# Squares of x summed on GpSimd, x's statistics requested earlier, and three early pieces inside the first unit, in a one-layer hybrid attention block

## The chip, the core and the metric

The kernel runs on one core of a Trainium2 chip. The metric is the device time of one execution in microseconds (us); the time shown is the median of three runs.

The core has these engines, each with a queue of its own that runs in order: TensorE (PE in the profile; its weight loads are PEld), VectorE (DVE), ScalarE (ACT), GpSimd (POOL) and SyncE (SP), which only issues the DMAs here.

## What is computed

One decoder layer for 256 tokens of 1024 features, all in float32:

```python
hn  = rmsnorm(x, g_attn)                    # mean of x*x over the features
qkv = hn @ w_in                             # 1024 x 3072: heads A, then heads B
ya  = rmsnorm(attention_a(qkv), g_out_a)    # 8 heads, dilated windows merged, ALiBi
yb  = rmsnorm(attention_b(qkv), g_out_b)    # 8 heads, causal (one block), ALiBi
h   = x + concat(ya, yb) @ w_out
h   = h + square(relu(rmsnorm(h, g_mlp) @ w_up)) @ w_down
h   = h + sigmoid(rmsnorm(h, g_ple) @ w_ple_gate + b) * (p @ w_ple_proj)
return rmsnorm(h, g_final)
```

## The kernel before

**Split operands.** Every large matmul is done with operands split in two parts, hi and lo, whose sum is the float32 value, as three matmuls: hi·hi, hi·lo, lo·hi (`mm3`, L207 to L211). A weight slab of 1 MB arrives as `raw`; ScalarE makes hi of a piece (L79), VectorE makes lo as raw minus hi (L86). A slab of the first unit has four pieces, 512 columns wide; a slab of the later attention units has two, 1024 wide. x is split in the same way into `aT` (L289 on ScalarE, L290 on VectorE).

**x's statistics.** The weights are multiplied with x not yet normalized, and the factor is applied to the products. `x_squares` squares x's eight feature blocks on ScalarE (L320, L323) and adds them up in `xsq` on VectorE (L324). `x_stats` sums over the features with small matmuls (L330), then VectorE makes the mean (L240) and GpSimd the reciprocal root (L241). `x_diag` (L339, VectorE) and `x_bcast` (L345 TensorE, L347 VectorE, L348 ScalarE) spread it over `rb`, with which q and k are multiplied when they leave PSUM.

**Order of the work.** For the attention part the order on TensorE, VectorE, ScalarE and GpSimd is the order in which the program emits the instructions (a manual schedule). A unit is a list of steps of matmuls. Its `inserts` say what is emitted after which step.
- Unit 1 of the list (here "the first unit") has 48 steps, six for each of the eight feature blocks k: two of v (0.70 us each) and four of q and k (0.36 us each). All its splits are emitted before its steps, in `first_splits`, block by block.
- The second unit (`slabs_in[2]`, 32 steps of q and k) has four pieces, made ahead of it: `early(0)` to `early(3)`. Here they are called hi(0), lo(0) to hi(3), lo(3).
- From the second unit on, a planner keeps a clock: each step adds its cost (0.36 or 0.681 us), and events (`at`, `within`) are emitted after the first step at whose end they are due. The clock is 0 at the end of the first unit. The clock places instructions in the queues; it delays none.
- While the second unit runs, the four pieces of the third (`slabs_in[5]`, called P0 to P3 here) are made; while the third runs, those of the fourth (`slabs_in[3]`, Q0 to Q3).

**One pair of heads (g, j).** `evac_qk` multiplies q and k with `rb` (mult, L362, VectorE), splits the result (qkhi L366, ScalarE; qklo L370, VectorE) and plans `scores` (L400, 12 matmuls). `scores` plans the softmax: `reduce` for each of two heads (L408, L411, VectorE: adds a table of distances and takes the maximum), `exp` for each head (L418, ScalarE), the reciprocal of the sums (L422, VectorE), `norm` (L429 on GpSimd and L431 on ScalarE), and the next pair's table, `make_bias` (L388, L390, GpSimd). It plans `turn` 7.4 after itself: six transposes (L451, TensorE), whose results are copied (L455, VectorE and ScalarE), and then `values` (L467, L468), whose result is split into y (L476, L485) and squared for the next norm (L478, L481, with an add on GpSimd, L482). The reciprocal is planned 4.7 and `norm` 4.8 after `scores`.

With n the number of the pair, scores of pair n are planned so:

```python
t = clock[0]
dt = 0.1 if n != 1 else 2.6
at(t + dt, mult)
at(t + dt + 0.7, hi)
at(t + dt + 1.4, lo)
at(max(t + dt + 3.2, 3.4 + 8.4 * n), lambda: scores(g, j), 0.75)
```

Of the kernel before, what the change touches and what calls it, by code (L numbers as in the profile page):

```python
# [10 lines left out]
F32 = mybir.dt.float32  # L11
# [3 lines left out]
ALU = mybir.AluOpType  # L15
PSUM = bass.MemoryType.PSUM

P = 128
S = 256
# [13 lines left out]
def block_kernel(ctx: ExitStack, tc: tile.TileContext, a: dict):  # L33
    nc = tc.nc
# [8 lines left out]
    def bank():  # L43
        n_ps[0] += 1
        return psum.tile([P, 512], F32, tag="ps", name=f"ps{n_ps[0]}")
# [65 lines left out]
    def at(t, f, cost=0.0):  # L111
        events.append((t, len(events), f, cost))
# [79 lines left out]
    def first_splits():  # L192
        for k in range(KT):
            if k in (0, 1, 2, 4):
                x_split(k, k + (1 if k < 2 else 2))
            sv, sq = (slabs_in[u][k // 4] for u in range(2))
            for part in (slice(0, 0.5), slice(0.5, 1)) if k == 0 else [slice(0, 1)]:
                for f in sv.halves(k % 4, part):
                    f()
            for f in sq.halves(k % 4):  # L200
                f()
            if k == 4:
                x_split(6, 8)
            if k:
                x_squares({1: range(2), 2: range(2, 4), 4: range(4, 8)}.get(k, ()))

    def mm3(ps, lhs, rhs, start, stop):  # L207

# [36 lines left out]
    ap = attn_pool.__enter__()  # L245
# [67 lines left out]
    xsq = ap.tile([P, S], F32, name="xsq")  # L313

    def x_squares(ks):

        for k in ks:
            x = x_rows(k, k + 1)[:, 0]
            if k == 0:
                nc.scalar.activation(xsq, x, AF.Square)  # L320
            else:
                sq = ap.tile([P, S], F32, tag="sq", name="sq", bufs=2)
                nc.scalar.activation(sq, x, AF.Square)  # L323
                nc.vector.tensor_tensor(xsq, xsq, sq, op=ALU.add)  # L324

    def sum_tokens(sums):

# [29 lines left out]
    def evac_qk(g, j, ps):  # L357
        d = pr[g, j] = {}

        def mult():  # L360
            d["raw"] = ap.tile([P, 2 * S], F32, tag="qk", name="qk", bufs=2)
            nc.vector.tensor_tensor(d["raw"], ps, rb, op=ALU.mult)  # L362

        def hi():
            d["hi"] = ap.tile([P, 2 * S], F32R, tag="qkhi", name="qkhi", bufs=3)
            nc.scalar.activation(d["hi"], d["raw"], AF.Copy)  # L366

        def lo():
            d["lo"] = ap.tile([P, 2 * S], F32R, tag="qklo", name="qklo", bufs=3)
            nc.vector.tensor_tensor(d["lo"], d["raw"], d["hi"].bitcast(F32), op=ALU.subtract)  # L370
            d["q"], d["k"] = ([t[:, i * S : (i + 1) * S] for t in (d["hi"], d["lo"])] for i in range(2))

        t = clock[0]
        n = NPAIR * g + j
        dt = 0.1 if n != 1 else 2.6
        at(t + dt, mult)
        at(t + dt + 0.7, hi)
        at(t + dt + 1.4, lo)
        at(max(t + dt + 3.2, 3.4 + 8.4 * n), lambda: scores(g, j), 0.75)

    biases = {}

    def make_bias(g, j):
        bias = biases[g, j] = ap.tile([P, 2, S], F32, tag="bias", name="bias", bufs=2)
        for h in range(2):
            head = 2 * j + h
            sl = SLOPES[2 * head + g]
            nc.gpsimd.tensor_scalar(bias[:, h], dist_b if g else dist_a, sl, 1.0, op0=ALU.mult, op1=ALU.mult)  # L388
            if g == 0:
                nc.gpsimd.tensor_tensor(bias[:, h], bias[:, h], logc, op=ALU.subtract)  # L390

    def scores(g, j):
        d = pr[g, j]

        ps = [bank(), bank()]
        for c, w, q0 in ((0, S, P), (S, P, 0)):
            for i, (a_, b_) in enumerate(((0, 0), (0, 1), (1, 0))):
                for h in range(2):
                    r = slice(h * HD, (h + 1) * HD)
                    last_mm[0] = nc.tensor.matmul(ps[h][:, c : c + w], d["q"][a_][r, q0 : q0 + P], d["k"][b_][r, :w],  # L400
                                                  start=i == 0, stop=i == 2)
        sc = ap.tile([P, 2, 3 * P], F32, tag="sc", name="sc", bufs=2)
        pb = d["p"] = ap.tile([P, 2, 3 * P], F32, tag="pb", name="pb", bufs=2)
        nm = ap.tile([P, 3, 4], F32, tag="nm", name="nm", bufs=3)
        parts = ((0, slice(P, 3 * P)), (1, slice(0, P)))

        def reduce(h):
            nc.vector.tensor_tensor_reduce(  # L408
                sc[:, h, P:], ps[h][:, :S], biases[g, j][:, h], 1.0, 3e38,
                op0=ALU.add, op1=ALU.min, accum_out=nm[:, 0, 2 * h : 2 * h + 1])  # L410
            nc.vector.tensor_tensor_reduce(  # L411
                sc[:, h, :P], ps[h][:, S : S + P], biases[g, j][:, h, P:], 1.0, 3e38,
                op0=ALU.add, op1=ALU.min, accum_out=nm[:, 0, 2 * h + 1 : 2 * h + 2])

        def exp(h):
            for i, sl in parts:
                c = slice(2 * h + i, 2 * h + i + 1)
                nc.scalar.activation(pb[:, h, sl], sc[:, h, sl], AF.Exp, bias=nm[:, 0, c], scale=-1.0,  # L418
                                     accum_out=nm[:, 1, c])

        def recip():
            nc.vector.reciprocal(nm[:, 2], nm[:, 1])  # L422

        def norm():
            for h in range(2):
                for i, sl in parts:
                    r = nm[:, 2, 2 * h + i : 2 * h + i + 1]
                    if i:
                        nc.gpsimd.tensor_scalar(pb[:, h, sl], pb[:, h, sl], r, 1.0, op0=ALU.mult, op1=ALU.mult)  # L429
                    else:  # L430
                        nc.scalar.activation(pb[:, h, sl], pb[:, h, sl], AF.Copy, scale=r)  # L431

        n = NPAIR * g + j
        within(0.75, lambda: reduce(0))
        within(1.4, lambda: reduce(1))
        within(1.9, lambda: exp(0))
        within(2.9, lambda: exp(1))
        within(4.7, recip)
        within(4.8, norm)
        if n < 7:  # L440
            within(0.8, lambda: make_bias((n + 1) // NPAIR, (n + 1) % NPAIR))
        within(7.4, lambda: turn(g, j), 0.7)
# [17 lines left out]
    def values(g, j):  # L460
        d = pr[g, j]
        ps = bank()
        v = vt[g]
        for h in range(2):
            cols = slice((2 * j + h) * HD, (2 * j + h + 1) * HD)
            o = ps[h * HD : (h + 1) * HD]
            nc.tensor.matmul(o[:, :S], v[:, 0, cols], d["pT"][h][:, :S], start=True, stop=False)  # L467
            last_mm[0] = nc.tensor.matmul(o[:, P:S], v[:, 1, cols], d["pT"][h][:, S:], start=False, stop=True)  # L468
        if j == 0 and g == 1:
            y1 = ap.tile([P, 2, NPAIR, S], F32R, tag="xy", name="y1")  # L470
            yT.append([y1[:, 0], y1[:, 1]])
        yh, yl = yT[g]
        gain = gv[:, 1, NPAIR * g + j : NPAIR * g + j + 1]

        def hi():
            nc.scalar.activation(yh[:, j], ps[:, :S], AF.Copy, scale=gain)  # L476
            if j == 0:
                nc.scalar.activation(ysum[g], ps[:, :S], AF.Square)  # L478
            else:
                sq = ap.tile([P, S], F32, tag="sq", name="sq", bufs=2)  # L480
                nc.scalar.activation(sq, ps[:, :S], AF.Square)  # L481
                nc.gpsimd.tensor_tensor(ysum[g], ysum[g], sq, op=ALU.add)  # L482

        def lo():
            nc.vector.scalar_tensor_tensor(yl[:, j], ps[:, :S], gain, yh[:, j].bitcast(F32),  # L485
                                           op0=ALU.mult, op1=ALU.subtract)

        within(1.0, hi)
        within(1.6, lo)
        if j == NPAIR - 1 and g == 0:  # L490
            within(3.6, lambda: y_stats(g), 0.3)
# [30 lines left out]
    def v_evac(g):  # L522
        for t in range(2):
            nc.scalar.activation(vt[g][:, t], held[g][t], AF.Copy, scale=xr["r"][:, t : t + 1])
# [45 lines left out]
    def early(n):  # L570

        return list(slabs_in[2][n // 2].halves(n % 2))
# [1 line left out]
    def b_evac():  # L574
        within(0.5, lambda: v_evac(1))

    def late_pieces():
        for n in (2, 3):
            hi, lo = early(n)
            at(1.3 * (n - 2), hi)  # L580
            at(1.3 * (n - 2) + 1.1, lo)

    units = [
        Unit(slabs_in[0] + slabs_in[1], first_steps,
             {33: [x_stats], 37: [x_diag] + early(0), 41: [x_bcast, lambda: make_bias(0, 0)], 43: early(1),
              48: [late_pieces, lambda: v_evac(0)]}),
        Unit(slabs_in[2], qk_steps(2, 0, 2), {14: [late_loads]}, 32, 0.36),
        Unit(slabs_in[5], v_steps(5, 1), {16: [b_evac]}, 16, 0.681),
        Unit(slabs_in[3], qk_steps(3, 1, 0), None, 32, 0.36),
# [313 lines left out]
```

## Time and profile before

| | us |
|---|---|
| median of three runs | 340.74 |
| lowest and highest of them | 340.59 to 340.94 |
| the profiled execution | 341.23 |
| its span in the profile | 339.4 |
| TensorE busy in it | 328.1 |

The profile is of one execution. The span is what the trace covers; the execution is 1.8 us longer than it. All instants below are microseconds from the start of the span. In a row of a timeline stand the start, the duration, the engine, the line, the operation, what is written and read, and how many instructions are merged; a bracket says how long the engine was idle before it and what ended that. Instructions that follow each other closely overlap a little in it, so the distance between starts is shorter than a duration.

### The profile page before, as it was taken

How to read it: one execution, taken by the hardware profiler on the slowest of the kernel's cores; microseconds unless marked ns; L12 is line 12 of the kernel's file. 1: busy time of each engine (PE TensorE's matmuls, PEld its weight loads, DVE VectorE, ACT ScalarE, POOL GpSimd, SP SyncE). 2: the span in 40 equal slices, each digit the busy share in tenths (PEclk: the TensorE clock that was granted, in tenths of full speed). 3: DMA queues.
4: the chain of work that ended last, by engine and by line, in shares of the span. 5: the costliest groups of instructions: out<-in, count | busy, mean ns of one | idle time of the engine just before them, and what ended most of it. 6: DMA issues, size and time to landing. Idle time of an engine off the chain costs nothing.

```text
span 339.4 us, 5168 instructions
## 1 busy us (share of the span) xinstructions
PE 328.1 (97%) x1932; PEld 281.8 (83%) x1932; DVE 233.1 (69%) x431; ACT 204.9 (60%) x400; POOL 43.1 (13%) x65
## 2 busy tenths in 40 slices
PE   8899989999999999999999999999999999999991
PEld 7789967899987788888888888888888888888890
DVE  3786987566765989879475686585755956658564
ACT  6785688847675968747364383554743836458421
POOL 0009057134122111000000000000000000000322
PEclk9999999999999999999999999999999999999997
DMA  7998883341433487735619437366193472700011
GB/s 197 358 356 289 315 280 143 112 193 50 145 136 126 140 317 245 289 126 186 250 62 322 172 109 265 126 239 254 21 352 124 146 257 95 249 0 1 2 62 62
DMA packets 10681, 60.84 MB, mean 179 GB/s; under 512 B 1184, under 2 KB 1952, under 8 KB 4128
## 3 DMA queue, kind: packets, MB, share of 16 engines
q1 hardware_dynamic: 10656, 60.51, 50.1%
q8 instruction: 15, 0.25, 0.3%
q14 instruction: 10, 0.08, 0.1%
HBM read 59.46 MB, written 1.05 MB: 178 GB/s over the span
## 4 chain that ended last, share of the span: by engine, by line
PE 84%; DVE 5%; DMA 4%; ACT 2%; issue 1%; SPq 1%; POOL 1%; POOLq 0%; DVEq 0%; ACTq 0%
PE ps L708 18%; PE ps L209 17%; PE ps L210 17%; PE ps L211 17%; PE ps L709 9%; DMA raw<-in_w_in 3%; PE ps L400 2%; DVE lo L86 2%; PE ps L451 2%; PE ps L467 1%; DMA xT<-in_xT 1%; PE ps L635 1%; DVE qklo L370 1%; ACT hi L79 1%; PE ps L468 1%
## 5 line engine op out<-in xcount | busy, mean ns | idle before, releaser
L86 DVE TENSOR_TENSOR lo<-raw,hi 128x1024 fp32r<-128x1024 f32 (+2 forms) x75 | 80.9, 1101 | 31.2 <-ACT hi L79 31.1
L708 PE MATMUL ps<-h,hi 128*128 128x512 f32 x256 | 90.9, 399 | 0.0
L79 ACT ACTIVATE hi<-raw 128x1024 fp32r<-128x1024 f32 (+2 forms) x75 | 69.3, 950 | 32.8 <-PE ps L211 27.0
L709 PE MATMUL ps<-h,lo 128*128 128x256 f32 x256 | 71.9, 281 | 0.0
L88 DVE SCALAR_TENSOR_TENSOR lo<-raw,head,hi 128x512 fp32r<-128x512 f32 x80 | 56.9, 746 | 9.6 <-ACT hi L81 9.6
L81 ACT ACTIVATE hi<-raw,head 128x512 fp32r<-128x512 f32 x80 | 52.8, 715 | 10.9 <-PE ps L211 5.5
L708 PEld LDWEIGHTS ps<-h,hi 128*128 128x128 f32 x256 | 48.1, 188 | 11.8
L209 PE MATMUL ps<-hi,u 128*128 128x512 f32 x128 | 50.3, 393 | 0.0
L211 PE MATMUL ps<-hi,u 128*128 128x512 f32 x128 | 49.9, 390 | 0.0
L210 PE MATMUL ps<-lo,u 128*128 128x512 f32 x128 | 49.9, 390 | 0.0
L709 PEld LDWEIGHTS ps<-h,lo 128*128 128x128 f32 x256 | 48.4, 189 | 0.2
L209 PE MATMUL ps<-x,hi 128*128 128x256 f32 x128 | 37.5, 293 | 0.0
L211 PE MATMUL ps<-x,lo 128*128 128x256 f32 x128 | 36.3, 283 | 0.2 <-DVE lo L86 0.2
L210 PE MATMUL ps<-x,hi 128*128 128x256 f32 x128 | 36.2, 283 | 0.0
L241 POOL TENSOR_TENSOR stat<-stat,mhalf 128x2 f32<-128x2 f32 x5 | 4.8, 960 | 225.0 <-DVE stat L240 225.0
L211 PEld LDWEIGHTS ps<-hi,u 128*128 128x128 f32 x128 | 24.0, 188 | 5.2
L209 PEld LDWEIGHTS ps<-hi,u 128*128 128x128 f32 x128 | 24.0, 188 | 5.0
L210 PEld LDWEIGHTS ps<-lo,u 128*128 128x128 f32 x128 | 24.1, 188 | 4.7
L209 PEld LDWEIGHTS ps<-x,hi 128*128 128x128 f32 x128 | 24.4, 191 | 1.5 <-issue 0.5
L211 PEld LDWEIGHTS ps<-x,lo 128*128 128x128 f32 x128 | 24.4, 191 | 0.4 <-DVE lo L86 0.4
L210 PEld LDWEIGHTS ps<-x,hi 128*128 128x128 f32 x128 | 24.4, 191 | 0.3
L689 ACT COPY r<-ps 128x256 f32<-128x256 f32 x32 | 11.7, 367 | 21.0 <-PE ps L709 20.9
(129 smaller groups left out, 511.3 us busy)
## 6 DMA issues: line engine op xcount, KB each, us to landing
raw<-in_w_up SPq DMA_DIRECT2D x16, 1024.0 KB, 5.1
raw<-in_w_down SPq DMA_DIRECT2D x16, 1024.0 KB, 4.8
raw<-in_w_in SPq DMA_DIRECT2D x8, 1024.0 KB, 5.4
raw<-in_w_out SPq DMA_DIRECT2D x4, 1024.0 KB, 4.8
raw<-in_w_gate SPq DMA_DIRECT2D x4, 1024.0 KB, 5.1
raw<-in_w_in SPq DMA_DIRECT2D x4, 512.0 KB, 9.3
raw<-in_w_in SPq DMA_DIRECT2D x7, 256.0 KB, 7.0
h_sb<-in_x SPq DMA_DIRECT2D x1, 1024.0 KB, 6.8
```

The lines of the kernel that those rows point to most:

```text
L79: nc.scalar.activation(h, r, AF.Copy)
L81: nc.scalar.activation(h, r, AF.Copy, scale=sc)
L86: nc.vector.tensor_tensor(l, r, h.bitcast(F32), op=ALU.subtract)
L88: nc.vector.scalar_tensor_tensor(l, r, sc, h.bitcast(F32), op0=ALU.mult, op1=ALU.subtract)
L209: nc.tensor.matmul(ps, lhs[0], rhs[0], start=start, stop=False)
L210: nc.tensor.matmul(ps, lhs[0], rhs[1], start=False, stop=False)
L211: last_mm[0] = nc.tensor.matmul(ps, lhs[1], rhs[0], start=False, stop=stop)
L400: last_mm[0] = nc.tensor.matmul(ps[h][:, c : c + w], d["q"][a_][r, q0 : q0 + P], d["k"][b_][r, :w], start=i == 0, stop=i == 2)
L451: nc.tensor.transpose(ps[:, c * P : (c + 1) * P], d["p"][:, h, c * P : (c + 1) * P], ident)
L689: nc.scalar.copy(b, ps[:, S:])
L708: nc.tensor.matmul(ps, s.hi[:, k % 4, col], aT2[2][:, k], start=k == 0, stop=False)
L709: last_mm[0] = nc.tensor.matmul(ps[:, S:], s.lo[:, k % 4, col], aT2[0][:, k], start=False, stop=k == KT - 1)
```

## The change

1. `x_squares`: the adds of the squares (L324) go from VectorE to GpSimd, and the temporary `sq` has three buffers and not two (also where y is squared).
2. The squares of blocks 6 and 7 are emitted after the splits of block 5 and not with those of block 4.
3. The statistics' parts are emitted sooner: `x_stats` after step 31 (was 33), `x_diag` after 34 (was 37), `x_bcast` after 38 (was 41).
4. The first pair's table, `make_bias(0, 0)`, is emitted with `x_diag`.
5. The pieces of the second unit: early(0) after step 34 (was 37), early(1) after 39 (was 43), early(2) after 44 (was planned at 0.0 and 1.1 on the clock); only early(3) is still planned, at 1.0 and 2.1 (was 1.3 and 2.4).
6. `v_evac(0)`, the copy of v out of PSUM on ScalarE, is planned at 1.6 and no longer emitted at the end of the first unit.
7. `scores` are planned 0.9 sooner: at 2.5 + 8.4 n, and the first pair's not before 2.4 after its mult is due.

```diff
             if k:
-                x_squares({1: range(2), 2: range(2, 4), 4: range(4, 8)}.get(k, ()))
+                x_squares({1: range(2), 2: range(2, 4), 4: range(4, 6), 5: range(6, 8)}.get(k, ()))
...
-                sq = ap.tile([P, S], F32, tag="sq", name="sq", bufs=2)
+                sq = ap.tile([P, S], F32, tag="sq", name="sq", bufs=3)
                 nc.scalar.activation(sq, x, AF.Square)
-                nc.vector.tensor_tensor(xsq, xsq, sq, op=ALU.add)
+                nc.gpsimd.tensor_tensor(xsq, xsq, sq, op=ALU.add)
...
-        at(max(t + dt + 3.2, 3.4 + 8.4 * n), lambda: scores(g, j), 0.75)
+        at(max(t + dt + (3.2 if n else 2.4), 2.5 + 8.4 * n), lambda: scores(g, j), 0.75)
...
-    def late_pieces():
-        for n in (2, 3):
-            hi, lo = early(n)
-            at(1.3 * (n - 2), hi)
-            at(1.3 * (n - 2) + 1.1, lo)
+    def late_piece():
+        hi, lo = early(3)
+        at(1.0, hi)
+        at(2.1, lo)
 
     units = [
         Unit(slabs_in[0] + slabs_in[1], first_steps,
-             {33: [x_stats], 37: [x_diag] + early(0), 41: [x_bcast, lambda: make_bias(0, 0)], 43: early(1),
-              48: [late_pieces, lambda: v_evac(0)]}),
+             {31: [x_stats], 34: [x_diag, lambda: make_bias(0, 0)] + early(0), 38: [x_bcast], 39: early(1),
+              44: early(2), 48: [late_piece, lambda: at(1.6, lambda: v_evac(0))]}),
```

## Rows read from the trace of the kernel before

**Rows 1.** The page: busy time, share of the span and instructions of each engine.

```profile
PE 328.1 (97%) x1932; PEld 281.8 (83%) x1932; DVE 233.1 (69%) x431; ACT 204.9 (60%) x400; POOL 43.1 (13%) x65
```

**Rows 2.** Waits of TensorE, 0 to 60 us: total us, times, longest.

```profile
PE ps L451 <- POOL pb L429: 1.1, 1, 1.1
...
PE ps L210 <- DVE lo L86: 0.5, 2, 0.2
```

**Rows 3.** Windows: length, then busy us of PE, PEld, DVE, ACT, POOL, clock, DMA.

```profile
60.00:320.00 260.00, 260.00 (x1459) 221.59 (x1458) 180.21 (x321) 156.51 (x297) 17.11 (x26) 1.00 0.47 166
```

**Rows 4.** Timeline of TensorE, 16 to 60 us.

```profile
21.11 0.28 PE L211 MATMUL ps<-x,lo 128*128 128x256 f32 x1
...
22.05 0.50 PE L210 MATMUL ps<-lo,x 128*128 128x512 f32 x1 [0.23 <-DVE lo L86]
22.39 0.40 PE L211 MATMUL ps<-hi,x 128*128 128x512 f32 x1
...
23.68 0.50 PE L330 MATMUL ps<-ones,xsq 128*128 128x1 f32 x4
...
27.66 0.61 PE L345 MATMUL ps<-diag,ones 128*128 128x128 f32 x4
...
34.96 0.39 PE L400 MATMUL ps<-qkhi 64*128 64x256 f32 x2
...
44.01 0.91 PE L451 MATMUL ps<-ident,pb 128*128 128x128 f32 x6 [1.11 <-POOL pb L429]
...
52.67 0.82 PE L451 MATMUL ps<-ident,pb 128*128 128x128 f32 x6
```

**Rows 5.** Timeline of ScalarE, 16 to 50 us.

```profile
18.62 0.71 ACT L323 ACTIVATE sq<-xT 128x256 f32<-128x256 f32 x2
...
20.66 3.22 ACT L79 ACTIVATE hi<-raw 128x512 fp32r<-128x512 f32 x6
...
38.17 0.51 ACT L418 ACTIVATE pb<-sc,nm 128x256 f32<-128x256 f32 x1 [0.15 <-DVE nm L408]
...
39.06 1.05 ACT L79 ACTIVATE hi<-raw 128x1024 fp32r<-128x1024 f32 x1
...
42.85 0.91 ACT L431 ACTIVATE pb<-pb,nm 128x256 f32<-128x256 f32 x2 [0.39 <-DVE nm L422]
```

**Rows 6.** Timeline of VectorE, 16 to 53 us.

```profile
18.56 0.88 DVE L290 SCALAR_TENSOR_TENSOR x<-xT,head,x 128x256 fp32r<-128x256 f32 x2
19.35 2.01 DVE L324 TENSOR_TENSOR xsq<-xsq,sq 128x256 f32<-128x256 f32 x4
21.30 3.70 DVE L86 TENSOR_TENSOR lo<-raw,hi 128x512 fp32r<-128x512 f32 x6
...
30.13 1.23 DVE L86 TENSOR_TENSOR lo<-raw,hi 128x1024 fp32r<-128x1024 f32 x1 [1.40 <-ACT hi L79]
...
33.44 1.22 DVE L370 TENSOR_TENSOR qklo<-qk,qkhi 128x512 fp32r<-128x512 f32 x1
...
42.29 0.17 DVE L422 RECIPROCAL nm<-nm 128x4 f32<-128x4 f32 x1
42.49 1.23 DVE L86 TENSOR_TENSOR lo<-raw,hi 128x1024 fp32r<-128x1024 f32 x1
...
46.35 0.41 DVE L408 CUSTOM_DVE_ANT_0 sc<-ps,bias 128x256 f32<-128x256 f32 x1
...
50.74 0.17 DVE L422 RECIPROCAL nm<-nm 128x4 f32<-128x4 f32 x1
```

**Rows 7.** Timeline of GpSimd, 16 to 60 us.

```profile
26.54 1.71 POOL L390 TENSOR_TENSOR bias<-bias,consts 128x256 f32<-128x256 f32 x1
...
28.83 0.74 POOL L390 TENSOR_TENSOR bias<-bias,consts 128x256 f32<-128x256 f32 x1
...
30.14 1.82 POOL L390 TENSOR_TENSOR bias<-bias,consts 128x256 f32<-128x256 f32 x1
...
32.53 1.58 POOL L390 TENSOR_TENSOR bias<-bias,consts 128x256 f32<-128x256 f32 x1
```

More of the change, by code (lines that the diff above doesn't have):

```diff
@@ L479, in hi @@
             else:
-                sq = ap.tile([P, S], F32, tag="sq", name="sq", bufs=2)
+                sq = ap.tile([P, S], F32, tag="sq", name="sq", bufs=3)
                 nc.scalar.activation(sq, ps[:, :S], AF.Square)
```

## Prediction, made before the changed kernel was run

> **What bounds the kernel now.** I read the page's busy times first, then TensorE's waits, the windows, and last the four engines' timelines between 16 and 53 us. TensorE is busy 97% of the span [rows 1]. Its waits lie almost all in the first 45 us: it waits a few tenths of a microsecond for lo pieces of VectorE and once 1.1 us for GpSimd's L429 [rows 2]; from 60 to 320 us it has no idle time [rows 3]. So the end moves only by what TensorE loses or no longer loses in the first 60 us, and every gain or loss there is carried unchanged to the end.
>
> Two of these losses are in reach of the change. At k=5 of the first unit the 512-column matmuls should go on at 21.23 (0.12 after 21.11) and 0.23 apart, so that L211 comes at 21.69; it comes at 22.39, because L210 waits for lo of k=5: 0.70 us lost [rows 4]. VectorE was adding four squares for 2.01 us just before that lo [rows 6]. And turn(0,0), the transposes of the first softmax, waits 1.11 us at 44.01 [rows 4]. Both gone would be 1.8 us.
>
> **What the adds cost on GpSimd.** The seven adds leave VectorE (four take 2.01 us there [rows 6], 0.43 to 0.50 each). On GpSimd one add of the same shape takes 0.74 us while VectorE is idle, but 1.82 us beside a lo piece: the lo runs from 30.13 to 31.36 and the add ends at 31.96, 0.60 after it [rows 6, 7]. It works the other way too: the add that ends at 34.11 holds back VectorE's L370, which was issued at 33.44 and ends at 34.66, 0.55 after the add, and takes 1.22 us [rows 6, 7] where six pieces of that shape pass in 3.70. So they take turns: a 512-wide lo and an add together cost 0.60 + 0.55 = 1.15 us.
>
> The Trainium skill says the same (SBUF — State Buffer, "Who interferes with whom": a VectorE instruction with two SBUF inputs and a GpSimd one that reads SBUF exclude each other for a whole instruction, the earlier one first); 1.82 against 0.74 agrees, and by that rule the sum is the one below, without it the first rival's. It speaks against the change also in Perfetto Trace Analysis, "Optimizing Scalar/DVE Operations": shifting work between these two engines may not help, because they share a read port.
>
> In the stretch of the last four adds VectorE has the six lo pieces to make. ScalarE squares k=4 and 5 from 18.62 as before [rows 5]; the next two squares now come behind hi of k=5, which no longer waits for the adds and starts at about 19.25. Then:
> - add 4 asks at 19.06, x's lo runs to 19.44 [rows 6], so it ends at 20.03; lo(v,5) 20.60, in time for 21.46, so the 0.70 us are saved;
> - add 5 ends 21.19, lo(q,5) 21.74, add 6 22.33, lo(v,6) 22.88, add 7 23.47.
>
> The sum L330 now stands behind step 31. TensorE gets there at 21.23 + 0.70 = 21.93 and waits until about 23.6, where the old one started at 23.68 two steps further on [rows 4]. Those two steps are 0.70 + 0.36 = 1.06 us of matmuls. TensorE is thus about 1.0 us behind (refills counted) where the first unit ends: 32.3 for 31.27. If adds never met a lo, each would take 0.82, the last end at 22.3 and L330 wait 0.4 us: 0.3 us ahead. That is the other bound.
>
> **The statistics are asked for sooner, not had sooner.** L240 stands on VectorE behind all lo pieces; the last of these ends at 25.24 for 25.00, so reciprocal root, diag and the first bias table all come 0.24 later. L345, behind step 38, comes at 27.58 for 27.66 [rows 4], now bound by TensorE. The copies to rb and hi(1) follow as before, and lo(1) 2.47 after L345, at 30.05 (30.13 before [rows 6]). Nothing is won here.
>
> **The three pieces put into the first unit.** lo(2), which stood behind mult(0), now stands before it. hi(2) is ready at 31.0 and its slab has long landed, but GpSimd's table add for (0,1) asked at 30.38 (30.14 before [rows 7]), waits for lo(1) and ends at 31.95; the 1024-wide lo(2) ends 1.08 after that, at 33.0. Then mult(0) 0.6, qkhi 0.63, qklo 0.69 and the hand-overs: 35.0. TensorE stands at scores(0,0), now behind 7 steps of its unit and not 10, at 32.3 + 2.5 = 34.8. So scores start at 35.05, 0.1 later than before (34.96 [rows 4]), three steps (1.07 us) of matmuls poorer. v_evac moves behind hi(3), where ScalarE waits anyhow; values need it much later. The third sq buffer only frees ScalarE. No DMA issue gets onto TensorE's path: the slabs of the third unit are asked for when lo(1) and lo(3) free their buffers, long before use.
>
> **turn(0,0).** Between scores and turn there are 19 steps now as before (7 to 26, 10 to 29), so the softmax has no more time. Behind qklo: hi(3) 1.05 to 35.25, lo(3) 1.23 to 36.5, mult(1) to 37.1, the first reduce at 37.0, qkhi(1) to 37.75, hi(P0) to 38.7, two exps of 0.89 each (38.17 to 39.06 [rows 5]) to 40.45. In the planner's times exp(1) (5.42) now stands before hi(P1) (5.90), which had gone first; lo(P1) (7.00) still stands before the reciprocal (7.22). So hi(P1) ends at 41.4, lo(P1) at 42.65, and the reciprocal starts at 42.6 for 42.29 [rows 6]. qklo(2) follows it and holds GpSimd's norm until 43.35; the transposes start 0.29 after such a lo (43.72 to 44.01 [rows 4, 6]): 43.64. TensorE is there at 42.85. It still waits 0.8 us, and at 43.64 has done 26 steps where it had done 29 at 44.01: 0.7 us behind.
>
> **turn(0,1).** Here is the largest term. norm(0) now comes (7.32) before hi(P2) (7.78), and lo(Q0) (15.72) before the second reciprocal (15.87), where each stood after. From the reciprocal at 42.6: norm 0.91 [rows 5] and hi(P2) to 44.85, lo(P2), held back by a table add, to 46.35, the copy to 46.8, lo(P3) to 48.0 or 48.5 (it meets the next table add within 0.1 us), reduces from 47.9 or 48.4 (46.35 before [rows 6]). From there: 0.45 to the exps, 0.89, y's hi and square 0.7 (two such take 0.71 [rows 5]), 0.89, hi(Q0) 1.05, lo(Q0) 1.15: 5.1 us to the reciprocal, where it was 4.39. So it starts at 53.0 to 53.5 for 50.74 [rows 6]; qklo(3) again goes ahead of the norm, 1.06 to the transposes: 54.05 to 54.55. TensorE gets there 8.66 + 0.39 after turn(0,0) (three steps of qk more, one of v less), at 52.7, and waits 1.4 to 1.9 us. At 54.3 it is one v step (0.69) short of what it had done at 52.67 [rows 4]: 54.3 + 0.69 - 52.67 = 2.3 us behind. For turn(0,2) the same count gives a chain of 8.8 us against 9.0 of matmuls: no further loss, but no slack either.
>
> **Rivals.**
> - The adds find the port free. Then L330 waits 0.4 us, rb comes 1.1 to 1.4 sooner, scores don't wait, the first reciprocal starts at about 41.0. turn(0,1) still follows it by 11.5 to 12: 52.8 + 0.69 - 52.67 = 0.8 us slower, 341.5. For it: 0.74 at 28.83 [rows 7]; against it: three of the four adds there met a lo and took 1.6 to 1.8.
> - Faster: the second softmax doesn't end last at turn(0,1), because VectorE, rid of 3 us of adds, hands it its reduces before the table adds get in; then only the saved 0.70 and the shorter wait at turn count, at best 1.8 us: 338.9. By the sum above the time is even when the first reciprocal starts at 40.2, so it must start below 39.5, or the second chain be 2 us shorter. For it: the second reciprocal was done 1.8 us ahead of its transposes before (50.91 to 52.67 [rows 4, 6]); against it: lo(Q0) and hi(P2) in its way.
> - VectorE keeps the port while its pieces are back to back (21.6 to 24.1). Then add 7 ends at about 25.5, L330 waits 3.6 us: some 4 us slower, 344.8. Against it: L370, which let the waiting add through [rows 6, 7].
> - Nothing measurable: the shorter waits and the new ones cancel.
>
> **How the numbers follow.** The profiled execution took 341.23 us (span 339.4), 0.5 more than the median 340.74; the 2.3 us are added to the median: 343.0. Chances: both turns wait as worked out, 342.0 to 344.2, 0.58; port free 0.15; faster 0.11; starved adds 0.08; cancelled 0.08. What this measurement tells from no change is about 0.2%, 0.68 us: 340.06 to 341.42. Of the port-free case a third falls inside that. Faster 0.12, same 0.15, slower 0.73. The range leaves out the faster case below and most of the starved one above: 340.1 to 344.6; the likeliest case's own is 342.0 to 344.2.
>
> **What would show it.** Right: the last adds of xsq on GpSimd 1.1 us apart, L330 waiting 1.6 us at 22, no wait for lo at 22.05, turn waiting about 0.8 us at 43.6 and about 1.6 us at 54. Wrong: adds of 0.74, or L451 with no wait at its second occurrence; the first to doubt are the two orders (lo(Q0) before the reciprocal, hi(P2) behind the norm) and who gets the port first.

## The result, and the profile after

The changed kernel takes 344.8 us (median of four executions, 343.3 to 345.6): 1.0103 times the time of the kernel before (95% interval 1.0086 to 1.0119). On the median of 340.74 us that is 344.2 us, 3.5 us more, where 2.3 were forecast. The sign and the places were right; one term was missing. The four executions differ in span and in mean granted clock (the share of its full speed that TensorE was given): 343.7 us at 0.989, 343.5 at 0.989, 342.4 at 0.993 and 341.5 at 0.993. The profile shown is that of the 343.7 us span. One execution of the kernel before beside the runs below, 465 us long at a granted clock of 0.657, is left out of every count.

TensorE's waits up to 70 us in the profile after (total, times, longest); these answer to [rows 2]:

```profile
PE ps L451 <- POOL pb L429: 2.4, 2, 1.7
PE ps L330 <- POOL xsq L324: 1.5, 1, 1.5
```

The wait for lo at k=5, 0.23 us at 22.05 before [rows 4], is gone. Two new ones are there: 1.5 us at the sum L330, and a second wait of an L451, 1.7 us. From 70 us on the list is empty, as it was before.

GpSimd's timeline after: the last four adds together, the last two of them each by itself, and the second norm:

```profile
19.27 4.28 POOL L324 TENSOR_TENSOR xsq<-xsq,sq 128x256 f32<-128x256 f32 x4 [3.97 <-ACT sq L323]
...
21.35 1.06 POOL L324 TENSOR_TENSOR xsq<-xsq,sq 128x256 f32<-128x256 f32 x1
...
22.49 1.05 POOL L324 TENSOR_TENSOR xsq<-xsq,sq 128x256 f32<-128x256 f32 x1
...
55.36 0.99 POOL L429 TENSOR_SCALAR pb<-pb,nm 128x128 f32<-128x128 f32 x2 [6.42 <-DVE nm L422]
```

VectorE's timeline after, to be read against [rows 6]:

```profile
19.98 5.32 DVE L86 TENSOR_TENSOR lo<-raw,hi 128x512 fp32r<-128x512 f32 x6 [0.45 <-ACT hi L79]
25.22 0.15 DVE L240 TENSOR_SCALAR stat<-ps 128x2 f32<-128x2 f32 x1
...
53.87 1.22 DVE L86 TENSOR_TENSOR lo<-raw,hi 128x1024 fp32r<-128x1024 f32 x1 [0.74 <-ACT hi L79]
55.01 0.17 DVE L422 RECIPROCAL nm<-nm 128x4 f32<-128x4 f32 x1
55.10 0.66 DVE L370 TENSOR_TENSOR qklo<-qk,qkhi 128x512 fp32r<-128x512 f32 x1
```

The four adds take 4.28 us and end at 23.55 (forecast: 23.47). An add alone takes 0.74 us [rows 7]; the last two take 1.06 and 1.05 and start 1.14 apart. VectorE's six lo pieces, which took 3.70 us [rows 6], take 5.32 beside them: each engine waits while the other's instruction runs. L240 starts at 25.22, 0.3 later than before, though the sum was requested two steps sooner. The second reciprocal (55.01) stands behind the lo at 53.87, and qklo at 55.10 then keeps the norm of 55.36 waiting.

TensorE's timeline after, which answers to [rows 4]:

```profile
21.15 0.28 PE L211 MATMUL ps<-x,lo 128*128 128x256 f32 x1
...
23.60 0.61 PE L330 MATMUL ps<-ones,xsq 128*128 128x1 f32 x4 [1.48 <-POOL xsq L324]
...
25.61 0.41 PE L209 MATMUL ps<-x,hi 128*128 128x256 f32 x1
25.82 0.41 PE L210 MATMUL ps<-x,hi 128*128 128x256 f32 x1
...
27.32 0.63 PE L210 MATMUL ps<-lo,x 128*128 128x512 f32 x1
...
29.20 0.61 PE L345 MATMUL ps<-diag,ones 128*128 128x128 f32 x4
...
45.17 0.91 PE L451 MATMUL ps<-ident,pb 128*128 128x128 f32 x6 [0.75 <-POOL pb L429]
...
56.05 0.90 PE L451 MATMUL ps<-ident,pb 128*128 128x128 f32 x6 [1.70 <-POOL pb L429]
```

The same stretch in windows (length, then busy us of PE, PEld, DVE, ACT, POOL, granted clock, DMA share and GB/s):

```profile
22.00:24.00 2.00, 0.52 (x5) 0.40 (x4) 2.00 (x2) 1.18 (x4) 1.47 (x2) 1.00 0.87 360
24.00:25.30 1.30, 1.30 (x9) 1.18 (x10) 1.30 (x4) 1.04 (x1) 0.00 (x0) 1.00 0.16 63
25.30:27.00 1.70, 1.70 (x11) 1.70 (x10) 0.87 (x4) 0.00 (x0) 1.38 (x3) 0.55 0.91 193
27.00:28.60 1.60, 1.60 (x6) 1.21 (x5) 0.96 (x1) 0.00 (x0) 1.54 (x1) 0.50 0.85 358
```

Here is what was not forecast. TensorE is busy for only 0.52 us between 22 and 24 us, waiting for xsq. From 23.60 it works at full clock until 25.3, and from there to 28.6 the granted clock is 0.55 and 0.50, the lower of its two levels: matmuls of 256 columns start 0.21 us apart, not 0.12, and one of 512 columns takes 0.63 us instead of 0.40. From L330 to L345 it takes 5.60 us; e3, e6 and e10 below, which keep their clock, need 4.06 to 4.08.

### The profile page after: what moved, and what is told of

Read it like the earlier page. It is cut to its first block, busy times and chain, and to the rows that moved or that the text cites. A ratio compares the mean times of both kernels' runs of the same rounds, so it can differ in the third digit from the quotient of the medians.

```text
span 343.7 us, 5170 instructions
## 1 busy us (share of the span) xinstructions
PE 329.7 (96%) x1932; PEld 283.3 (82%) x1932; DVE 233.4 (68%) x424; ACT 204.2 (59%) x400; POOL 47.8 (14%) x72
## 3 DMA queue, kind: packets, MB, share of 16 engines
HBM read 59.46 MB, written 1.05 MB: 176 GB/s over the span
## 4 chain that ended last, share of the span: by engine, by line
PE 81%; ACT 5%; DVE 4%; DMA 2%; issue 2%; SPq 2%; POOL 2%; POOLq 0%; DVEq 0%; ACTq 0%
PE ps L707 17%; PE ps L209 17%; PE ps L211 16%; PE ps L210 16%; PE ps L708 9%; DMA raw<-in_w_in 2%; ACT hi L79 2%; DVE lo L86 2%; PE ps L400 1%; PE ps L451 1%; SPq L265 1%; PE ps L467 1%; POOL xsq L324 1%; ACT pb L418 1%; PE ps L634 1%
## 5 line engine op out<-in xcount | busy, mean ns | idle before, releaser
L86 DVE TENSOR_TENSOR lo<-raw,hi 128x1024 fp32r<-128x1024 f32 (+2 forms) x75 | 84.4, 1148 | 35.7 <-ACT hi L79 35.5
L211 PE MATMUL ps<-hi,u 128*128 128x512 f32 x128 | 49.9, 390 | 0.0
L211 PE MATMUL ps<-x,lo 128*128 128x256 f32 x128 | 36.7, 286 | 0.2 <-DVE lo L86 0.2
L211 PEld LDWEIGHTS ps<-hi,u 128*128 128x128 f32 x128 | 24.0, 188 | 5.2
L211 PEld LDWEIGHTS ps<-x,lo 128*128 128x128 f32 x128 | 24.7, 193 | 0.4 <-DVE lo L86 0.4
```

Source lines behind the costliest of these rows:

```text
L86: nc.vector.tensor_tensor(l, r, h.bitcast(F32), op=ALU.subtract)
L211: last_mm[0] = nc.tensor.matmul(ps, lhs[1], rhs[0], start=False, stop=stop)
```

## The experiments

Each kernel was timed in five rounds beside the kernel before on the same chip, whose medians there were 340.9 to 341.1 us. The runs are named in the table below by their numbers.

**e1: the adds back on VectorE.** The changed kernel with this edit:

```diff
-                nc.gpsimd.tensor_tensor(xsq, xsq, sq, op=ALU.add)
+                nc.vector.tensor_tensor(xsq, xsq, sq, op=ALU.add)
```

> The changed kernel, with the seven adds of xsq given back to VectorE; all else stays changed. Theory P (the port makes the adds late, and the earlier planning makes the softmax of pair 1 late): add 7 now ends at about 22.3 instead of 23.55, so the sum L330 waits 0.3 to 0.5 us instead of 1.5, the clock keeps its full grant between 25 and 29 us, and the pair-0 reciprocal starts at about 41.5 instead of 44.1. turn(0,0) and turn(0,1) still wait (0.8 to 1.5 us each), because their order is unchanged: about 342.0 us, between the two kernels, still 0.2 to 0.5% slower than before. Rival A (the place of the adds is the whole cause): 340.7 us or less, no wait at the second L451.

Measured: 343.2 us, ratio 1.0063 (1.0040 to 1.0086). TensorE's waits there:

```profile
21.99 0.61 PE L330 MATMUL ps<-ones,xsq 128*128 128x1 f32 x4 [0.34 <-DVE xsq L324]
...
42.06 0.90 PE L451 MATMUL ps<-ident,pb 128*128 128x128 f32 x6 [0.40 <-POOL pb L429]
...
52.95 0.90 PE L451 MATMUL ps<-ident,pb 128*128 128x128 f32 x6 [1.71 <-POOL pb L429]
```

The wait at the sum shrinks to 0.34 us, turn(0,0) waits 0.40, and turn(0,1) waits 1.71 as in the changed kernel. The place of the adds is not the whole cause: without them on GpSimd more than half of the loss stays, a little more than expected.

**e2: the adds moved, and two squares later.** The kernel before, with the first two edits of the change and nothing else:

```diff
-                x_squares({1: range(2), 2: range(2, 4), 4: range(4, 8)}.get(k, ()))
+                x_squares({1: range(2), 2: range(2, 4), 4: range(4, 6), 5: range(6, 8)}.get(k, ()))
...
-                nc.vector.tensor_tensor(xsq, xsq, sq, op=ALU.add)
+                nc.gpsimd.tensor_tensor(xsq, xsq, sq, op=ALU.add)
```

(with three buffers for sq.)

> The kernel before, with the adds on GpSimd, three buffers and the squares of blocks 6 and 7 behind the splits of block 5; everything else as before. Theory P: the wait for lo at 22.05 is gone (0.7 us won), the sum L330, still behind step 33, waits about 0.6 us at 23.0 to 23.6, the two cancel; no fall of the clock; turn(0,0) waits about 1.0 us as before: 340.4 to 341.1 us, no measurable change. Rival A (the place of the adds is the whole cause): 342 us or more.

Measured: 341.1 us, ratio 1.0001 (0.9987 to 1.0015). Its waits at the sum and at the first turn:

```profile
22.69 0.61 PE L330 MATMUL ps<-ones,xsq 128*128 128x1 f32 x4 [0.32 <-POOL xsq L324]
...
43.19 0.91 PE L451 MATMUL ps<-ident,pb 128*128 128x128 f32 x6 [1.18 <-POOL pb L429]
```

Behind step 33 the same late adds cost 0.32 us, and the saved wait for lo pays for it. The adds on GpSimd, with the two later squares, neither win nor lose.

**e5: only scores planned sooner.** The kernel before with the one line of the planning:

```diff
-        at(max(t + dt + 3.2, 3.4 + 8.4 * n), lambda: scores(g, j), 0.75)
+        at(max(t + dt + (3.2 if n else 2.4), 2.5 + 8.4 * n), lambda: scores(g, j), 0.75)
```

> The kernel before, with the earlier planning of scores alone (2.5 + 8.4 n, and 2.4 for the first pair). Theory P: the planned orders behind scores(0,0) become those of the changed kernel: scores(0,0) wait about 0.9 us for their q and k, turn(0,0) waits about 0.5 us, and turn(0,1) waits 1.7 us, since the second reciprocal stands behind the fourth unit's first lo: 1.8 us slower than before, 0.4 to 0.7%. Rival A (the adds on GpSimd and the earlier statistics are what costs, and scores planned sooner only use the time): no slower than before, and no wait at the second L451.

Measured: 343.4 us, ratio 1.0069 (1.0047 to 1.0092). TensorE:

```profile
35.80 0.39 PE L400 MATMUL ps<-qklo,qkhi 64*128 64x256 f32 x2 [0.45 <-DVE qklo L370]
...
44.02 0.91 PE L451 MATMUL ps<-ident,pb 128*128 128x128 f32 x6 [0.42 <-POOL pb L429]
...
54.92 0.90 PE L451 MATMUL ps<-ident,pb 128*128 128x128 f32 x6 [1.71 <-POOL pb L429]
```

This line alone carries about two thirds of the loss. The 1.71 us at the second turn are there without any add of xsq on GpSimd and with the statistics where they were. The wait at scores (0.45) is half of what was expected.

**e3: the reverse.** The changed kernel, with that line as before.

> The changed kernel, with the planning of scores as before (3.2 after the multiplication, 3.4 + 8.4 n). Theory P: L330 still waits 1.5 us and the clock may still fall behind it, turn(0,0) waits about 0.9 us, and turn(0,1) no longer waits (1.7 us in the changed kernel), because the second reciprocal is planned before the fourth unit's first lo again: about 1.7 us faster than the changed kernel, 342 to 343 us. Rival A: no different from the changed kernel, 344.3 us.

Measured: 342.8 us, ratio 1.0051 (1.0031 to 1.0071), executions from 341.0 to 344.4. TensorE, and a window of the stretch in which the changed kernel's clock was low:

```profile
24.00 0.61 PE L330 MATMUL ps<-ones,xsq 128*128 128x1 f32 x4 [1.42 <-POOL xsq L324]
...
28.07 0.60 PE L345 MATMUL ps<-diag,ones 128*128 128x128 f32 x4
...
45.21 0.91 PE L451 MATMUL ps<-ident,pb 128*128 128x128 f32 x6 [0.82 <-POOL pb L429]
...
53.87 0.81 PE L451 MATMUL ps<-ident,pb 128*128 128x128 f32 x6
```

```profile
26.00:28.00 2.00, 2.00 (x14) 1.78 (x13) 1.39 (x3) 0.00 (x0) 1.83 (x3) 1.00 0.90 254
```

The second L451 no longer waits; the sum still does, 1.42 us. The granted clock is full behind it in this profile. All of the change but this one line costs 0.5%; its edits 4 to 6 were not tried one by one.

**e6: two instructions exchanged.** The changed kernel, with the reciprocal planned 0.2 sooner:

```diff
-        within(4.7, recip)
+        within(4.5, recip)
```

> The changed kernel, with the reciprocal planned 4.5 and not 4.7 after scores. Only one pair of instructions changes places on any engine: the second reciprocal (L422) and the lo of the fourth unit's first piece (L86) on VectorE. Theory P: the second reciprocal starts about 2 us sooner, GpSimd's norm of the first head is done before that lo, that of the second head behind it, so the wait at the second L451 falls from 1.7 us to 0.4, with some 0.5 us more between its two halves: 0.8 to 1.2 us faster than the changed kernel (0.25 to 0.35%). Rival B (the second softmax is late for its reduces, not for that order): no change, the wait stays 1.7 us.

Measured: 343.0 us, ratio 1.0063 (1.0040 to 1.0086); the changed kernel beside it took 345.5 (e8). VectorE around the exchanged pair, and TensorE:

```profile
50.78 0.17 DVE L422 RECIPROCAL nm<-nm 128x4 f32<-128x4 f32 x1
51.61 1.24 DVE L86 TENSOR_TENSOR lo<-raw,hi 128x1024 fp32r<-128x1024 f32 x1 [0.66 <-ACT hi L79]
```

```profile
22.79 0.61 PE L330 MATMUL ps<-ones,xsq 128*128 128x1 f32 x4 [1.85 <-POOL xsq L324]
...
26.87 0.60 PE L345 MATMUL ps<-diag,ones 128*128 128x128 f32 x4
...
51.94 0.27 PE L451 MATMUL ps<-ident,pb 128*128 128x128 f32 x1
52.55 0.84 PE L451 MATMUL ps<-ident,pb 128*128 128x128 f32 x5 [0.34 <-ACT pb L431]
```

The reciprocal now stands before the fourth unit's first lo, and the 1.71 us at the second turn become none for the first transpose and 0.34 for the rest. The theory of the planned order holds: one exchanged pair takes away 1.4 us of waiting at that turn. What it is worth in time is less (0.7 us, worked out behind the table below); most of the 2.5 us to the changed kernel is the clock's fall, which this profile doesn't have even behind a wait of 1.85 us at the sum (4.08 us from L330 to L345).

**e8: the changed kernel again.**

> The changed kernel itself, beside the others on one chip. Theory C (the grant falls to half for some 3.5 us behind the 1.5 us wait at L330 in some executions and not in others): the waits are the same again (1.5, 0.75 and 1.7 us), and if the grant is full between 25 and 29 us in this profile, its span is 341.5 to 342.3 us instead of 343.7. Rival D (the grant falls in every execution): the same fall again, a span near 343.7.

Measured: 345.5 us (344.1 to 346.0), ratio 1.0123 (1.0099 to 1.0147). The windows behind the wait:

```profile
24.00:26.00 2.00, 2.00 (x12) 1.85 (x12) 1.33 (x4) 0.53 (x1) 0.59 (x1) 0.78 0.40 90
26.00:28.00 2.00, 2.00 (x10) 1.81 (x9) 1.76 (x3) 0.00 (x0) 1.83 (x3) 0.50 0.83 295
```

The waits are the same and the clock falls again, to 0.78 and 0.50. It does not fall in every execution: the first measurement has two at 0.989 and two at 0.993, and of the six here one stands at 0.997.

**e4 and e10: something for TensorE to do.** The changed kernel, with matmuls on zeros in front of the sum (13 in e4, 26 in e10; their result is not used):

```diff
         ps = bank()
+        if sums is xsq:
+            for _ in range(26):
+                nc.tensor.matmul(ps[:, 256 : 256 + P], warm, warm, start=True, stop=True)
```

> The changed kernel, with 13 matmuls of a tile of zeros (128x128, as at the kernel's start, about 0.1 us each) in front of the sum L330, into an unused part of its bank: TensorE has something to do in most of the 1.5 us for which it waits for xsq, and the sum comes no earlier. Theory C (the idle 1.5 us make the grant fall to half between 25 and 29 us, which is the 1 to 2 us that the forecast lacks): the grant stays full, the end lies 2.3 us behind before, about 343.0 us, and the runs scatter less than the changed kernel's 343.3 to 345.6. Rival D (the grant falls for another reason, or the time between 25 and 29 us isn't on the path): 344 us or more, the same scatter.

> The changed kernel, with 26 matmuls of zeros in front of L330, which at the 0.06 us that each took in the run with 13 fill the whole wait of 1.5 us. L330 starts as late as in the changed kernel, TensorE is only not idle. Theory C: the grant stays full in every execution, and what is left is the late chain: 2.3 to 2.7 us slower than before, about 343.6 us, 1.5 us faster than the changed kernel in the executions where its grant fell. Rival D (the fall doesn't come from the idle time): a mean of 345 us as in the changed kernel.

Measured: e4 344.5 us, ratio 1.0101 (1.0081 to 1.0120), e10 344.1 us, ratio 1.0090 (1.0073 to 1.0108). The 13 matmuls took 0.06 us each, so e4 filled only half of the wait and its times tell little. e10 fills it (the added lines move L330 to L333, L345 to L348 and L451 to L454):

```profile
20.68 0.28 PE L211 MATMUL ps<-x,lo 128*128 128x256 f32 x1
...
21.51 1.62 PE L331 MATMUL ps<-warm 128*128 128x128 bf16 x26
23.11 0.60 PE L333 MATMUL ps<-ones,xsq 128*128 128x1 f32 x4
...
27.17 0.60 PE L348 MATMUL ps<-diag,ones 128*128 128x128 f32 x4
...
43.23 0.91 PE L454 MATMUL ps<-ident,pb 128*128 128x128 f32 x6 [0.75 <-POOL pb L432]
...
54.11 0.90 PE L454 MATMUL ps<-ident,pb 128*128 128x128 f32 x6 [1.70 <-POOL pb L432]
```

```profile
22.00:24.00 2.00, 2.00 (x27) 1.80 (x25) 2.00 (x3) 1.49 (x3) 1.05 (x1) 1.00 0.89 369
...
26.00:28.00 2.00, 2.00 (x14) 1.76 (x13) 1.65 (x3) 0.00 (x0) 1.92 (x2) 1.00 0.91 360
```

The sum still starts behind the last add, with hardly any idle time ahead of it; the clock stays full, and none of the six executions has a mean granted clock under 0.992. (Their scatter, 1.1 us for 1.9 and 2.2 of the changed kernel, says little: the kernel before scatters by 1.7 beside them.) All of the chain's waits remain (0.75 and 1.70 us). So this is the change without the fall of the clock: about 3 us slower than before by the medians, of which 2.3 were forecast.

**e9: the sum back behind step 33.** The changed kernel with

```diff
-             {31: [x_stats], 34: ...
+             {33: [x_stats], 34: ...
```

> The changed kernel, with the sum L330 back behind step 33; the rest of the change stays. Theory C (the wait of 1.5 us in front of L330 brings the fall of the grant to half, seen in both profiles of the changed kernel, which costs 1.5 us from L330 to L345: 5.60 us instead of 4.08): the wait falls to about 0.4 us, the grant stays full, L345 comes 0.5 to 1 us sooner than without the fall and 2.2 us sooner than with it, turn(0,1) still waits about 1.7 us: 342.4 to 343.2 us, no execution above 344. Rival D (the fall has to do with the changed order elsewhere): the same fall with the small wait, 344 us or more.

Measured: 343.3 us, ratio 1.0076 (1.0050 to 1.0101), executions from 342.2 to 344.9. The sum and the second turn:

```profile
23.30 0.61 PE L330 MATMUL ps<-ones,xsq 128*128 128x1 f32 x4 [0.31 <-POOL xsq L324]
...
53.61 0.90 PE L451 MATMUL ps<-ident,pb 128*128 128x128 f32 x6 [1.71 <-POOL pb L429]
```

The wait is 0.31 us and the clock full in this profile, as expected. The median lies just above the expected 342.4 to 343.2, and one execution above 344, so the bound on single executions failed. That execution has a mean granted clock of 0.989 and another one 0.987, where the other four have 0.993 or 0.994: the clock seems to have fallen in these two all the same.

**e7: the useful part, and the first turn later.** The kernel before, with the squares of blocks 6 and 7 and their adds behind the splits of block 5, on VectorE, and one number more:

```diff
-                x_squares({1: range(2), 2: range(2, 4), 4: range(4, 8)}.get(k, ()))
+                x_squares({1: range(2), 2: range(2, 4), 4: range(4, 6), 5: range(6, 8)}.get(k, ()))
...
-        within(7.4, lambda: turn(g, j), 0.7)
+        within(7.4 if n else 8.6, lambda: turn(g, j), 0.7)
```

> The kernel before, with only the useful part of the change, on VectorE (squares of blocks 6 and 7 and their adds behind the splits of block 5, three sq buffers), and with turn(0,0) planned 8.6 instead of 7.4 after its scores, so that TensorE has three more steps and the next scores to do before it waits for the first softmax. Theory P: the wait for lo at k=5 (0.7 us) and the wait of turn(0,0) (1.1 us) go, nothing new waits: 1.5 to 1.8 us faster than before, 0.45 to 0.55%. Rival E (what is taken away there comes back at the next softmax, or at the sum): within 0.2% of before.

Measured: 338.6 us (338.3 to 339.3), ratio 0.9930 (0.9910 to 0.9949): faster than both kernels, by somewhat more than expected. All that TensorE waits for up to 70 us in it:

```profile
PE ps L209 <- ACT hi L79: 1.2, 1, 1.2
PE ps L220 <- DVE mhalf L229: 1.0, 1, 1.0
PE ps L210 <- DVE lo L86: 0.2, 1, 0.2
PE ps L211 <- DVE lo L86: 0.2, 1, 0.2
```

These waits are those of the start, for the first loads and their splits. The two losses that the prediction saw in reach of the change, at lo of k=5 and at the first turn, are gone, and nothing has taken their place.

The table counts in one more way, which leaves out that the first loads do not land at the same instant in every execution: from the start of the last matmul of block 4 (L211 at 21.11 before [rows 4], 21.15 in the changed kernel, 20.68 in e10) to the end of the span, less the 318.3 us that this takes in the kernel before. Its last column has the executions with a mean granted clock of 0.990 or less.

| kernel | wait at L330 | first turn | second turn | ratio to before | from block 4 to the end, against before (us) | at 0.990 or less |
|---|---|---|---|---|---|---|
| before | 0 | 1.11 | 0 | 1 | 0 | 1 of 45 |
| changed | 1.48 | 0.75 | 1.70 | 1.0103 | 4.3 | 2 of 4 |
| changed again (e8) | 1.45 | 0.74 | 1.71 | 1.0123 | 4.4 | 5 of 6 |
| changed, adds on VectorE (e1) | 0.34 | 0.40 | 1.71 | 1.0063 | 1.7 | 2 of 6 |
| changed, scores as before (e3) | 1.42 | 0.82 | 0 | 1.0051 | 0.7 | 4 of 12 |
| changed, 13 fillers (e4) | 0.70 | 0.76 | 1.71 | 1.0101 | 2.9 | 1 of 6 |
| changed, 26 fillers (e10) | 0 (filled) | 0.75 | 1.70 | 1.0090 | 2.8 | 0 of 6 |
| changed, reciprocal first (e6) | 1.85 | 0.75 | 0.34 | 1.0063 | 2.2 | 2 of 7 |
| changed, sum behind 33 (e9) | 0.31 | 0.41 | 1.71 | 1.0076 | 2.1 | 2 of 6 |
| before, adds on GpSimd (e2) | 0.32 | 1.18 | 0 | 1.0001 | 0 | 0 of 12 |
| before, scores sooner (e5) | 0 | 0.42 | 1.71 | 1.0069 | 2.4 | 0 of 6 |
| before, split squares, turn later (e7) | 0 | 0 | 0 | 0.9930 | -2.0 | 0 of 6 |

The waits don't add up to the times, since a turn planned sooner waits with fewer steps done.

Of the profiles only those of the changed kernel and of e8 have the clock's fall. Without it the change costs 2.8 us (e10). Of these, 2.1 go with scores planned sooner (e3 keeps 0.7; e5's 2.4 have 0.2 from a later load), 1.1 with the adds on GpSimd (e1 keeps 1.7), and 0.7 with the exchanged pair (e6 keeps 2.2); they overlap, so they add up to more. Of the 2.0 us that e7 wins, 0.7 are there when L345 starts, so they come from the later squares, and 1.3 arise behind it, from the later turn.

The last column says more of the fall than single profiles do. Of the changed kernel, 7 of 10 executions stand at 0.990 or less (one of them at 0.938 with a span like the others', which isn't explained); their spans are 1.5 us longer in the mean than those of the other three. In e1, e3, e6 and e9 too such executions are 1.3 to 1.5 us longer than the rest of the same kernel. That is what the fall costs in the profiles. So e3 and e6 seem to lose the clock in some executions, though not in the one profiled, and so do e1 and e9, with waits of 0.34 and 0.31 us at the sum in their profiles; where in the span it fell there isn't recorded.

## Why the prediction was right, and what it lacked

**The adds take turns with the lo pieces: right.** Forecast: the last add ends at 23.47, L330 starts at about 23.6. Measured: 23.55 and 23.60, the last adds 1.14 us apart, as in the forecast. The Trainium skill has this as a rule (SBUF — State Buffer, "Who interferes with whom": a VectorE instruction with two SBUF inputs and a GpSimd one that reads SBUF lock each other out, the earlier one first); the trace agrees, with 1.05 us for an add against 0.74 alone. The first rival, adds that find the port free, falls, and so does the third, adds that starve: a waiting add got in after every lo.

**Asked for sooner, not had sooner: right.** L240 came 0.3 us later than before (0.24 forecast).

**turn(0,0) still waits: right.** 0.8 us forecast, 0.75 measured.

**turn(0,1) is the largest term: right.** A wait of 1.4 to 1.9 us was forecast, 1.70 measured, and e6 shows that it hangs on the order that the step named: lo(Q0) before the second reciprocal. In the runs whose clock stayed full the instants agree too. In e10, whose block 4 ends 0.4 us sooner than before, L330 starts at 23.11 and the turns at 43.23 and 54.11: 20.1 and 31.0 us behind it, where 20.0 and 30.7 were forecast. turn(0,2) waits for nothing, as forecast. The second rival, in which VectorE without adds hands over its reduces in time, falls with e1 and e5: the second turn waits 1.71 us with the adds on VectorE and even in the old order of the statistics.

**The size: too small, by a missing term.** The step that failed is "TensorE is thus about 1.0 us behind where the first unit ends": it counted the wait at L330 and nothing after it. In both profiles of the changed kernel the granted clock then falls to its lower level for some 3.5 us, and L345 comes 5.60 us after L330, not 4.08. As L345 waits for nothing but TensorE, all 1.5 us go into the chain: the turns are 1.5 and 1.7 us late (45.17 and 56.05 for 43.64 and 54.3). e10 ties it to TensorE standing idle at the sum: with the wait filled, none of six executions has a mean clock of 0.990 or less, where 7 of 10 of the changed kernel do. That is a large part of why 344.2 us stands at the upper end of the likeliest case (342.0 to 344.2).

**What stays open.** Without the fall the change still costs 2.8 us counted from block 4, for 2.3 forecast. Of the missing 0.5, half is there when the second turn starts in e10 (33.4 us behind that matmul, for 33.2 forecast: 54.3 less 21.11); the rest arises behind that turn without any wait, and its cause wasn't found. And the length of the wait at the sum does not settle whether the clock falls: it fell behind 1.48 and 1.45 us and not behind 1.42 and 1.85 in the profiles (e3, e6), and it seems to fall in some executions of e1 and e9, whose profiles have short waits there. What else decides it is not shown.

## What to carry to other kernels

When a transpose or a sum waits on the engine that is the bottleneck, look first whether that engine has other work that could stand before it: planning the first turn later by 1.2, with the two late squares moved behind the next splits, gained 0.7%, while hurrying everything ahead of the turn lost 1%. An add that leaves VectorE for GpSimd isn't gone when both read two SBUF operands: here an add and a lo piece together took 1.14 us, in turns. And a planned time moved by 0.9 reorders queues elsewhere; write down which neighbours change places (here a lo piece and a reciprocal, planned at 15.72 and 15.87 on the planner's clock) before trusting the gain.

## What the runs showed of the hardware

In two profiles of the changed kernel the granted clock of TensorE fell to half, 1.5 to 1.8 us after it had gone back to work behind an idle time of only 1.45 to 1.48 us, stayed there for some 3.5 us, and came back while TensorE was busy all along; the price is 1.5 us (5.60 us for 4.06 to 4.08 from L330 to L345). It did not fall behind waits of 1.42 and 1.85 us in the profiles of e3 and e6, and of the changed kernel itself 3 of 10 executions show no sign of it. With matmuls on zeros in the gap (26, 0.06 us apart) none of six executions has a mean granted clock of 0.990 or less, against 7 of 10 without them.

A GpSimd add and a VectorE lo piece, each with two SBUF operands, took turns when both engines had work waiting: 1.14 us for the two, with neither engine starved.
